# Modulation products on column quarters, 64 slots for the first expert, and the expert order ahead of its gather

## The chip, the cores and the metric

The kernel runs on one core of a Trainium2 chip. The metric is device time of one execution in microseconds (us), a median of several runs. Five engines work side by side: TensorE (PE; its weight loads are shown as PEld), VectorE (DVE), ScalarE (ACT), GpSimd (POOL) and SyncE (SP), which here does little but issue loads from memory. A program has one queue of instructions for each engine; engines wait for each other by semaphores.

## The reference, cut to what matters

Three transformer layers on 256 tokens of 1024 columns, in float32. The change is in layer 1 (and in a helper that layer 3 uses too). Layer 1 computes a modulation of six parts from one vector `c`, a mixer, and a mixture of 32 experts, of which each token takes four:

```python
mod = jax.nn.silu(c) @ w_ada[l] + b_ada[l]                  # [1024] @ [1024, 6144]
sh1, sc1, gt1, sh2, sc2, gt2 = [m[:, None, :] for m in jnp.split(mod, 6, axis=-1)]
h = rms_norm(x, g_pre_mix[l]) * (1 + sc1) + sh1
y = hybrid_mixer(h, ...)
x = x + gt1 * rms_norm(y, g_post_mix[l])
h = rms_norm(x, g_pre_ffn[l]) * (1 + sc2) + sh2
y = moe_ffn(h, w_router[l], ...)      # top_k of 32, softmax, per expert: @ w_mlp1, swiglu, @ w_mlp2
x = x + gt2 * rms_norm(y, g_post_ffn[l])
```

Layer 2 has another mixer and a dense feed-forward part, layer 3 a modulation of its own, attention, and 32 smaller experts. The router decides at run time how many of the 256 tokens an expert gets.

## The kernel before

**Modulation.** `Ada` holds `silu(c)` as 8 columns of 128 (`c[:, k]`), and works on `w_ada` in 24 tiles of 1 MiB, each with 8 blocks (k) of 128 rows by 256 columns, for 256 values of the modulation. `Ada.tile(n, pe)` does the first `pe` blocks on TensorE, as a product with one column of `c` (L301, a single row of 256 as the result), and the others on VectorE as multiplications and additions into an accumulator of 128 rows (L304, L306). `Ada.columns` turns the result into two columns of 128: the accumulator and the row are summed by small products with ones (L325), and VectorE adds the bias (L329). Layer 1's parts (1, 0) come with four blocks on each engine, ahead of the mixer; the parts 2, 4 and 3 entirely on VectorE, woven into the mixer; the last four tiles by `Fill` (L365), as single rows on TensorE between the steps of norm and router. Layer 3 calls `Ada.tile` with all 8 blocks on TensorE for six of its tiles, and leaves the others to VectorE.

**Order of the experts.** Expert 0 is always done first. The 31 others are put into places 1 to 31 by how many tokens they got. `Order.keep` copies the mask of the choices (on GpSimd, L1171), `Order.make` counts, ranks (a matrix `perm`), sorts the biases by place (L1231) and then writes the list of expert numbers `ids` (L1194 on TensorE, L1195 on VectorE). `Order.expert` reads an entry of it into a register of SP (L1221), which the address of a load needs.

**Slots.** A place has room for `CAPS` tokens: places 0 to 4 have 128 slots, the next eleven 64, the others 32. `gather` collects the tokens of a group of places by products with a 0/1 matrix (L1305, L1306). What exceeds a place's slots is done by `overflow1` at the end, behind a branch.

**Experts.** Each has 12 weight tiles of 1 MiB: 8 of `w_mlp1`, 4 of `w_mlp2`, issued by SP (L134) into a ring of 12 slots. `Expert1.product` (L1556) makes the 4 products of a tile, the tokens being stationary and the weights moving; with 64 slots the two halves of the result lie on two column halves of the engine, with 32 slots on four column quarters. Between the tiles `step` and `advance` weave the gathers of the next group, the activation, and the scatter of the expert before. Ten tiles of expert 0 are issued ahead of the first load that needs `ids`.

**Order of the work.** In most of the mixer a scheduler orders each engine's queue; from the norm after it to the first expert, and again from the second expert on, the order on TensorE, VectorE and ScalarE is that of the code.

Of the kernel before, what the change touches and what calls it, by code (L numbers as in the profile page):

```python
# [31 lines left out]
class Kern:  # L32
# [21 lines left out]
    def constants(self):  # L54

        nc, pool = self.nc, self.perm
        self.ident = self.cload("ident", [P, P], pool)
# [220 lines left out]
class Ada:  # L278
# [13 lines left out]
    def tile(self, n, pe, wv=None):  # L292


        K, nc = self.K, self.K.nc
        wv = (K.wtile(K.a[self.w][n]) if wv is None else wv).rearrange("p (k n) -> p k n", k=KD)
        terms, ps = [], None
        if pe:
            ps = K.bank()[0:1, :256]
            for k in range(pe):  # L300
                nc.tensor.matmul(ps, self.c[:, k:k + 1], wv[:, k], start=k == 0, stop=k == pe - 1)  # L301
        if pe < KD:
            acc = self.pool.tile([P, 256], F32, tag="acc", name="acc")
            nc.vector.tensor_scalar(acc, wv[:, pe], self.c[:, pe:pe + 1], None, op0=ALU.mult)  # L304
            for k in range(pe + 1, KD):
                nc.vector.scalar_tensor_tensor(acc, wv[:, k], self.c[:, k:k + 1], acc, op0=ALU.mult, op1=ALU.add)  # L306
            terms.append((acc, K.ones[:, 0:1]))
        return n, terms, ps

    def column(self, n, terms, row):  # L310
        weave(self.columns(n, terms, row))

    def columns(self, n, terms, row):

        K, nc = self.K, self.K.nc
        if row is not None:
            acc = self.pool.tile([P, 256], F32, tag="acc", name="acc")[0:1]
            nc.scalar.copy(acc, row)
            terms.append((acc, K.ones[0:1, 0:1]))
        yield  # L320
        yield
        ps = K.bank()
        for j in range(2):
            for i, (acc, one) in enumerate(terms):
                nc.tensor.matmul(ps[:, j:j + 1], acc[:, 128 * j:128 * j + 128], one, start=i == 0, stop=i == len(terms) - 1)  # L325
        for _ in range(6):
            yield
        m = slice(2 * n, 2 * n + 2)
        nc.vector.tensor_add(self.mod[:, m], ps[:, :2], self.b[:, m])  # L329
# [5 lines left out]
    def tiles(self, ns, pe=lambda n: 0):  # L335
        last = None
        for n in ns:
            t = self.tile(n, pe(n % 4))
# [6 lines left out]
    def steps(self, parts, pe=lambda n: 0):  # L345
# [3 lines left out]
class Fill:  # L349
# [9 lines left out]
    def go(self, m):  # L359
        K = self.ad.K  # L360
        for _ in range(min(m, KD * len(self.ns) - self.next)):
            i, k = divmod(self.next, KD)
            if k == 0:
                self.ps.append(K.bank()[0:1, :256])
# [2724 lines left out]
```

## Time and profile before

| | us |
|---|---|
| median of 3 runs | 2215.63 |
| lowest, highest | 2211.54, 2216.04 |
| profiled execution | 2217.96 |
| its span in the trace | 2216.1 |

| engine | busy, us | share |
|---|---|---|
| PE | 2008.4 | 91% |
| DVE | 994.4 | 45% |
| ACT | 639.2 | 29% |
| POOL | 135.8 | 6% |

The stages in the trace: modulation and first norm 0 to 44.5, mixer to 165.1, norm, router and first gather to 197, experts of layer 1 to 1173, layer 2 and the mixer of layer 3 to about 1900, its experts to 2187, and the end. A share of busy time over the whole span is a mean over these stages; the rows below are read stage by stage. "Idle before" is the time in which an engine did nothing just ahead of an instruction, with what ended it. The clock of TensorE is given as a share of its full speed (PEclk).

### The profile page before, as it was taken

To read this page: it belongs to the slowest core of one execution; us is meant where nothing else is said; L and a number is where in the kernel's file an instruction comes from. 1 tells how busy PE (TensorE), PEld (TensorE's weight loads), DVE (VectorE), ACT (ScalarE), POOL (GpSimd) and SP (SyncE) were. 2 spreads that over 40 slices of the span, in tenths; PEclk is the share of its full clock that TensorE was granted. 3 is DMA by queue.
4 is the path that set the end of the run, shared out by engine and by line. 5 is a ranking of instruction groups with operands and counts; after the bars stand their busy time and mean duration, and the time that the engine had idled before them with its cause. 6 is when DMAs were issued, how large, how long until landed. Compare 5 with 4: busy or idle time off the path is not lost. (4 is left out here: it accounts for less than half of the span.)

```text
span 2216.1 us, 31702 instructions
## 1 busy us (share of the span) xinstructions
PE 2008.4 (91%) x12454; PEld 1255.3 (57%) x12454; DVE 994.4 (45%) x2096; ACT 639.2 (29%) x1162; POOL 135.8 (6%) x199
## 2 busy tenths in 40 slices
PE   7899999988988898879976978999999999899996
PEld 4785434332423243223415956999778999556664
DVE  5783322221222222222225997788565854323334
ACT  3553101110101001010104583444454543322221
POOL 4000000000000000000000001000200000000000
PEclk9999999999999999999997988999999999899998
DMA  7665899999999999999995523577442554799991
GB/s 290 238 246 203 362 420 410 420 419 419 420 419 419 419 420 419 419 419 420 419 419 212 201 84 133 213 281 284 164 149 101 196 177 147 297 362 395 397 399 43
DMA packets 97807, 680.08 MB, mean 307 GB/s; under 512 B 11760, under 2 KB 14064, under 8 KB 16112
## 3 DMA queue, kind: packets, MB, share of 16 engines
q1 hardware_dynamic: 94752, 671.00, 76.1%
q0 software_dynamic: 2320, 6.41, 1.0%
q8 instruction: 102, 1.67, 0.3%
q10 hardware_dynamic: 576, 0.53, 0.1%
q14 instruction: 57, 0.47, 0.1%
HBM read 675.79 MB, written 2.11 MB: 306 GB/s over the span
## 5 line engine op out<-in xcount | busy, mean ns | idle before, releaser
L1556 PE MATMUL bank<-w,xg 128*32 128x512 f32 (+2 forms) x2048 | 460.3, 626 | 65.1 <-DMA w<-w_mlp 64.9
L1556 PEld LDWEIGHTS bank<-w,xg 128*32 128x32 f32 (+2 forms) x2048 | 131.2, 135 | 323.6 <-issue 188.7
L167 DVE TENSOR_TENSOR whl<-w,whl 128x1024 fp32r<-128x1024 f32 (+1 forms) x211 | 251.4, 1199 | 136.2 <-ACT whl L166 135.9
L166 ACT CAST whl<-w 128x1024 fp32r<-128x1024 f32 (+1 forms) x219 | 221.5, 1029 | 229.9 <-PE bank L417 99.9
L1556 PE MATMUL bank<-w,a 128*32 128x512 f32 (+2 forms) x1024 | 256.0, 610 | 24.7 <-DMA w<-w_mlp 24.7
L1586 ACT COPY us<-bank 128x512 f32<-128x512 f32 x64 | 37.5, 585 | 527.8 <-PE bank L1556 527.8
L1641 DVE TENSOR_TENSOR sg<-bank,b1cols 128x128 f32<-128x128 f32 (+2 forms) x64 | 25.6, 400 | 361.6 <-PE bank L1593 200.4
L1556 PEld LDWEIGHTS bank<-w,a 128*32 128x32 f32 (+2 forms) x1024 | 67.3, 131 | 141.4 <-issue 93.7
L1352 DVE TENSOR_TENSOR moe<-moe,bank 128x512 f32<-128x512 f32 x128 | 82.3, 684 | 119.4 <-PE bank L1347 108.4
L415 PE MATMUL bank<-hh,whl 128*128 128x256 f32 x448 | 129.0, 288 | 0.0
L417 PE MATMUL bank<-hh,whl 128*128 128x256 f32 x448 | 126.8, 283 | 2.1 <-DVE whl L167 2.1
L416 PE MATMUL bank<-hl,whl 128*128 128x256 f32 x448 | 126.8, 283 | 0.0
L2944 PE MATMUL bank<-w,xg 128*64 128x256 f32 x1024 | 118.5, 384 | 0.0
L306 DVE SCALAR_TENSOR_TENSOR acc<-w,siluc,acc 128x256 f32<-128x256 f32 x234 | 115.0, 499 | 4.5
L417 PE MATMUL bank<-xh,whl 128*128 128x256 f32 x400 | 113.1, 283 | 2.2 <-DVE whl L167 2.2
L415 PE MATMUL bank<-xh,whl 128*128 128x256 f32 x400 | 113.2, 284 | 0.8 <-ACT xh L1860 0.8
L416 PE MATMUL bank<-xl,whl 128*128 128x256 f32 x400 | 113.2, 283 | 0.0
L2762 DVE TENSOR_TENSOR moe<-moe,bank 128x512 f32<-128x512 f32 x60 | 39.8, 684 | 149.9 <-PE bank L2989 149.9
L2944 PEld LDWEIGHTS bank<-w,xg 128*64 128x64 f32 x1024 | 70.8, 138 | 37.7 <-issue 3.6
L417 PEld LDWEIGHTS bank<-hh,whl 128*128 128x128 f32 x448 | 85.0, 190 | 3.1 <-DVE whl L167 3.1
L415 PEld LDWEIGHTS bank<-hh,whl 128*128 128x128 f32 x448 | 85.3, 190 | 0.9 <-issue 0.6
L416 PEld LDWEIGHTS bank<-hl,whl 128*128 128x128 f32 x448 | 85.2, 190 | 0.6 <-issue 0.5
(721 smaller groups left out, 3519.8 us busy)
## 6 DMA issues: line engine op xcount, KB each, us to landing
w<-w_mlp SPq DMA_DIRECT2D x384, 1024.0 KB, 19.8
w<-w SPq DMA_DIRECT2D x96, 1024.0 KB, 7.7
w<-w_ada SPq DMA_DIRECT2D x48, 1024.0 KB, 5.4
w<-w_in SPq DMA_DIRECT2D x48, 1024.0 KB, 4.8
w<-w_ff SPq DMA_DIRECT2D x32, 1024.0 KB, 4.9
w<-w_out SPq DMA_DIRECT2D x12, 1024.0 KB, 4.9
w<-cmp_w SPq DMA_DIRECT2D x4, 1024.0 KB, 4.7
w<-w_ret_o SPq DMA_DIRECT2D x4, 1024.0 KB, 4.8
```

The lines of the kernel that those rows point to most:

```text
L166: nc.scalar.copy(h, src)
L167: (eng or nc.vector).tensor_tensor(l, src, h.bitcast(F32), op=ALU.subtract)
L306: nc.vector.scalar_tensor_tensor(acc, wv[:, k], self.c[:, k:k + 1], acc, op0=ALU.mult, op1=ALU.add)
L415: nc.tensor.matmul(out, w.h[k][:, c], x.h[:, k], start=first and k == 0, stop=False)
L416: nc.tensor.matmul(out, w.h[k][:, c], x.l[:, k], start=False, stop=False)
L417: nc.tensor.matmul(out, w.l[k][:, c], x.h[:, k], start=False, stop=last and k == nk - 1)
L1352: nc.vector.tensor_add(out[:, t, c], out[:, t, c], ps[n])
L1556: self.K.nc.tensor.matmul(out[n % self.banks][r:r + cap], x[:, k], w[:, k % 2, 512 * n:512 * n + 512], start=k < m, stop=k >= KD - m)
L1586: (nc.scalar.copy, nc.vector.tensor_copy)[n](us[:, n], u[n])
L1641: nc.vector.tensor_tensor(o, ps, v.rearrange("p (c a) -> p c a", a=1).broadcast_to([P, 4, cap]), op=ALU.add)
L2762: nc.vector.tensor_add(out[:, k:k + 2], out[:, k:k + 2], ps)
L2944: nc.tensor.matmul(self.u[64 * n:64 * n + 64], self.xg[:, k], w[:, j, n], start=k == 0, stop=k == KD - 1)
```

## The change

Four things. (1) A modulation tile of layer 1 is no longer shared with VectorE nor done as a single row. All 8 blocks are products on TensorE, `dot`, with the column of `c` broadcast to 32 columns: block k writes the 32 rows of quarter k modulo 4 of a result of 128 by 256. ScalarE copies this result (`kept`), two products with the identity turn it, and VectorE sums the four quarters and adds the bias. `Fill` does the same. The identity is loaded ahead of the first tile's columns. Layer 3's tiles that are done on TensorE become quarters too; its others stay on VectorE. (2) Place 0 has 64 slots instead of 128, and `Order.make` writes its limit accordingly. (3) `Order.keep` and the first part of `Order.make` come directly after the choice of the experts; `ids` is written ahead of expert 0's gather, the sorted biases after it. (4) The splits of the tokens for the gather (`tok.l_of`) and the first steps of that gather are put in other places between the last modulation products.

```diff
@@ class Ada
-        if pe:
-            ps = K.bank()[0:1, :256]
-            for k in range(pe):
-                nc.tensor.matmul(ps, self.c[:, k:k + 1], wv[:, k], start=k == 0, stop=k == pe - 1)
-        if pe < KD:
-            acc = self.pool.tile([P, 256], F32, tag="acc", name="acc")
-            nc.vector.tensor_scalar(acc, wv[:, pe], self.c[:, pe:pe + 1], None, op0=ALU.mult)
-            for k in range(pe + 1, KD):
-                nc.vector.scalar_tensor_tensor(acc, wv[:, k], self.c[:, k:k + 1], acc, op0=ALU.mult, op1=ALU.add)
-            terms.append((acc, K.ones[:, 0:1]))
-        return n, terms, ps
+        if pe:
+            ps = K.bank()[:, :256]
+            for k in range(KD):
+                self.dot(ps, wv, k)
+            return n, True, ps
...
+    def dot(self, ps, wv, k):
+        r = slice(32 * (k % 4), 32 * (k % 4) + 32)
+        self.K.nc.tensor.matmul(ps[r], self.c[:, k:k + 1].broadcast_to([P, 32]), wv[:, k], start=k < 4, stop=k >= KD - 4)
...
+    def kept(self, ps):
+        acc = self.pool.tile([P, 256], F32, tag="acc", name="acc")
+        self.K.nc.scalar.copy(acc, ps)
+        return acc
...
         for j in range(2):
-            for i, (acc, one) in enumerate(terms):
-                nc.tensor.matmul(ps[:, j:j + 1], acc[:, 128 * j:128 * j + 128], one, start=i == 0, stop=i == len(terms) - 1)
+            if quarters:
+                transpose_to(K, ps[:, 128 * j:128 * j + 128], acc[:, 128 * j:128 * j + 128])
+            else:
+                nc.tensor.matmul(ps[:, j:j + 1], acc[:, 128 * j:128 * j + 128], K.ones[:, 0:1], start=True, stop=True)
...
+            nc.vector.reduce_sum(self.mod[:, m], ps[:, :256].rearrange("p (j g r) -> p j g r", j=2, g=4)[:, :, :, 0], axis=AX.X)
+            nc.vector.tensor_add(self.mod[:, m], self.mod[:, m], self.b[:, m])
@@ class Fill, go
-                self.ps.append(K.bank()[0:1, :256])
-            K.nc.tensor.matmul(self.ps[i], self.ad.c[:, k:k + 1], self.w[i][:, k], start=k == 0, stop=k == KD - 1)
+                self.ps.append(K.bank()[:, :256])
+            self.ad.dot(self.ps[i], self.w[i], k)
@@ mix1
-    mods = ad.steps((1, 0), lambda n: 4)
+    mods = ad.steps((1, 0), True)
+    K.ident = K.cload("ident", [P, P], K.perm)
...
-        weave(att, linear(), ad.steps((2, 4)), also)
+        weave(att, linear(), ad.steps((2, 4), True), also)
...
-        weave(output(), ad.steps((3,)))
+        weave(output(), ad.steps((3,), True))
@@
-CAPS = [WIDE] * WIDES + [NARROW] * NARROWS + [SLIM] * (E1 - WIDES - NARROWS)
+CAPS = [NARROW] + [WIDE] * (WIDES - 1) + [NARROW] * NARROWS + [SLIM] * (E1 - WIDES - NARROWS)
@@ Order.make
-        bias_columns(K, b1, self.perm.bitcast(F32), self.b1)
-
-        yield
+        yield
+
         ps = K.bank()
         nc.tensor.matmul(ps[0:1, :n], K.iota_p[:n], perm, start=True, stop=True)
         nc.vector.tensor_copy(self.ids, ps[0:1, :n])
+        yield
+        bias_columns(K, b1, self.perm.bitcast(F32), self.b1)
+        yield
...
+        nc.vector.tensor_scalar(more, pos, 0.0, float(NARROW - WIDE), op0=ALU.is_equal, op1=ALU.mult)
+        nc.vector.tensor_tensor(cap, cap, more, op=ALU.add)
@@ the mixture of experts, layer 1
+            order.keep(best.mask)
             R = Routes(K, rt, best.mask, E1, lambda: tok.l_of(0))
+            made = order.make(K, rt, R, b1)
+            next(made)
             fill.go(32)
-            order.keep(best.mask)
-            tok.l_of(1)
...
             step()
+            tok.l_of(1)
+            next(made)
             tok.l_of(2)
             tok.l_of(3)
+            step(4)
             fill.columns()
             fill.copy()
             fill.columns()
...
-            step(3)
...
-                            made = order.make(K, rt, R, b1)
                             next(made)
```

TensorE's queue around the first expert, before (L1067 to L1071 are the routing, L365 the last modulation tiles, L1305 and L1306 expert 0's gather, L1556 its products, L1179 and L1181 the counts of `Order.make`, L1231 its biases; a row's last numbers are the result's shape and how often it stands):

```order
L1071 MATMUL bank<-topm,ones 1x32
L365 MATMUL bank<-w,siluc_90 1x256 x11
L325 MATMUL bank<-ones,acc 128x1 x8
L1305 MATMUL bank<-oh,tokh 128x128
L1306 MATMUL bank<-oh,tokl 128x128
...
L1556 MATMUL bank<-w,xg 128x512 x4
...
L1179 MATMUL bank<-mask_1688,ones 128x32 x2
L1181 MATMUL bank<-ones,mask_1688 128x1 x2
L1556 MATMUL bank<-w,xg 128x512 x2
L1231 MATMUL bank<-perm,b_360 128x32 x16
```

The same place of the same queue after (L1080 routing, L1188 and L1190 the counts, L309 the modulation quarters, L1202 the list `ids`, L1318 and L1319 the gather, L556 the turning, L1571 expert 0's products, L1244 the biases):

```order
L1080 MATMUL bank<-topm,ones 1x32
L1188 MATMUL bank<-mask_1708,ones 128x32 x2
L1190 MATMUL bank<-ones,mask_1708 128x1 x2
L309 MATMUL bank<-w,siluc_90 32x256 x11
L1202 MATMUL bank<-perm,iota_p 1x32
L1318 MATMUL bank<-oh,tokh 128x64
L1319 MATMUL bank<-oh,tokl 128x64
...
L556 MATMUL bank<-ident,acc 128x128 x8
L1571 MATMUL bank<-w,xg 64x512 x4
...
L1244 MATMUL bank<-perm,b_344 128x32 x8
```

The counts and the list stand behind the routing and ahead of the gather, where before the counts stood behind the fourth of expert 0's products and the list (L1194) further back.

TensorE's queue in the mixer, before (L325 are the sums of a modulation tile that VectorE accumulated, L1781, L794 and L804 the mixer's own work):

```order
L417 MATMUL bank<-hh,whl 128x256
L325 MATMUL bank<-ones,acc 128x1 x2
L1781 MATMUL bank<-bmr,flip 128x512
L794 MATMUL bank<-state,qe_615 64x128 x4
...
L804 MATMUL bank<-v,AT 64x128 x16
L325 MATMUL bank<-ones,acc 128x1 x2
```

The same place after (L309 are the 8 quarter products of a modulation tile, L556 its turning):

```order
L425 MATMUL bank<-hh,whl 128x256
L309 MATMUL bank<-w,siluc_90 32x256 x8
L556 MATMUL bank<-ident,acc 128x128 x2
L1796 MATMUL bank<-bmr,flip 128x512
...
L813 MATMUL bank<-v,AT 64x128 x16
L309 MATMUL bank<-w,siluc_90 32x256 x8
```

A tile's 8 products and two turning products stand between full-width products of the mixer, in place of two products with ones.

VectorE's queue at the softmax of the mixer's attention, before (L696, L697 and L700 are its sum, reciprocal and scaling, L304 and L306 modulation tiles):

```order
L304 TENSOR_SCALAR acc<-w,siluc_90 128x256
L306 SCALAR_TENSOR_TENSOR acc<-w,siluc_90,acc 128x256 x4
L696 TENSOR_TENSOR sm<-sm,es 128x8
L306 SCALAR_TENSOR_TENSOR acc<-w,siluc_90,acc 128x256
L697 RECIPROCAL sm<-sm 128x8
...
L700 TENSOR_SCALAR s<-s,sm 128x128 x4
```

And after (L336 and L337 are the sum of the quarters and the bias):

```order
L336 TENSOR_REDUCE modw_ada<-bank 128x2
L337 TENSOR_TENSOR modw_ada<-modw_ada,b_ada 128x2
L705 TENSOR_TENSOR sm<-sm,es 128x8
L706 RECIPROCAL sm<-sm 128x8
L709 TENSOR_SCALAR s<-s,sm 128x128 x4
```

The accumulations between the three steps of the softmax are gone from this queue.

## Rows read from the trace of the kernel before

**Rows 1.** Windows by stage: window, length, busy per engine, PEclk, DMA share, GB/s.

```profile
0.00:44.50 44.50, 32.10 (x134) 17.10 (x134) 25.81 (x64) 13.75 (x28) 17.58 (x33) 0.98 0.88 314
44.50:165.10 120.60, 112.81 (x818) 96.18 (x819) 94.92 (x227) 63.76 (x128) 13.42 (x16) 0.95 0.66 237
165.10:197.00 31.90, 30.54 (x182) 17.96 (x180) 16.07 (x50) 13.55 (x31) 1.05 (x3) 0.98 0.91 362
197.30:229.30 32.00, 32.00 (x134) 18.69 (x134) 6.91 (x30) 6.64 (x19) 2.10 (x2) 0.91 0.03 5
229.30:1171.70 942.40, 843.23 (x4342) 314.89 (x4340) 230.82 (x526) 106.99 (x226) 74.87 (x126) 0.97 1.01 418
1927.50:2187.00 259.50, 255.40 (x1879) 162.54 (x1878) 79.62 (x177) 60.02 (x162) 0.00 (x0) 0.99 0.86 341
```

**Rows 2.** Waits of SP, 160 to 260: line, waited for, total us, times, longest.

```profile
SPq L1221 <- DVE ids L1195: 47.3, 1, 47.3
```

**Rows 3.** Timeline around 226 (start, length, work), and loads issued 226 to 230.

```profile
226.40 0.18 DVE L1195 CAST ids<-bank 1x32 int32<-1x32 f32 x1 [0.94 <-PE bank L1194]
227.77 33.22 SPq L134 DMA_DIRECT2D w<-w_mlp  x16
...
DMA to landing us min/median/max: 4.9/7.7/10.6
```

**Rows 4.** Windows within the experts of layer 1, columns as in rows 1.

```profile
300.00:350.00 50.00, 50.00 (x174) 20.81 (x173) 12.75 (x27) 4.24 (x9) 5.95 (x6) 1.00 1.01 418
...
450.00:500.00 50.00, 41.31 (x280) 16.21 (x279) 11.41 (x27) 7.50 (x17) 2.45 (x6) 0.91 1.01 419
```

**Rows 5.** PE groups by shape, 229 to 1175: rows*columns, moving, count | busy, mean ns.

```profile
L1556 PE MATMUL bank<-w,xg 128*64 128x512 f32 x704 | 167.8, 603 | 30.1 <-DMA w<-w_mlp 30.1
L1556 PE MATMUL bank<-w,xg 128*32 128x512 f32 x1024 | 145.9, 647 | 33.1 <-DMA w<-w_mlp 32.9
L1556 PE MATMUL bank<-w,xg 128*128 128x512 f32 x279 | 124.7, 598 | 1.9 <-DMA w<-w_mlp 1.9
L1556 PE MATMUL bank<-w,a 128*32 128x512 f32 x512 | 97.8, 618 | 14.7 <-DMA w<-w_mlp 14.7
```

**Rows 6.** Expert 0's products alone (L1556): window, length, PE and PEld busy.

```profile
196.99:251.99 55.00, 39.86 (x81) 14.78 (x81) 0.95 0.43 175
```

**Rows 7.** End of the first stage: PE timeline, and a window as in rows 1.

```profile
36.37 1.89 PE L301 MATMUL bank<-w,siluc 128*1 128x256 f32 x8
...
44.51 0.58 PE L417 MATMUL bank<-hh,whl 128*128 128x256 f32 x1 [2.08 <-DVE whl L167]
...
35.00:44.50 9.50, 6.30 (x35) 4.43 (x34) 9.29 (x24) 6.16 (x13) 3.48 (x3) 0.89 0.63 225
```

**Rows 8.** Mixer, 44.5 to 165.1: two groups as in rows 5, one wait of PE.

```profile
L306 DVE SCALAR_TENSOR_TENSOR acc<-w,siluc,acc 128x256 f32<-128x256 f32 x84 | 38.4, 479 | 1.1
L325 PE MATMUL bank<-ones,acc 128*128 128x1 f32 x40 | 5.2, 235 | 0.0
PE bank L548 <- ACT s L702: 6.0, 1, 6.0
```

**Rows 9.** Routing, 165 to 197: a PE group, and the PE timeline.

```profile
L548 PE MATMUL bank<-ident,hf 128*128 128x128 f32 x16 | 2.2, 280 | 0.0
...
187.98 4.91 PE L365 MATMUL bank<-w,siluc 128*1 128x256 f32 x22
```

**Rows 10.** Layer 3: timeline of PE and DVE, and a wait of SP from 1935 on.

```profile
1569.16 3.61 PE L301 MATMUL bank<-w,siluc 128*1 128x256 f32 x16
...
1571.47 0.81 DVE L2337 TENSOR_SCALAR xn<-xn,lnmv,lnrs 128x1024 f32<-128x1024 f32 x1
...
1902.84 5.17 PE L301 MATMUL bank<-w,siluc 128*1 128x256 f32 x16 [4.98 <-DMA w<-w_ada]
...
1952.19 3.62 PE L301 MATMUL bank<-w,siluc 128*1 128x256 f32 x16
...
SPq L134 <- PE bank L2944: 145.6, 55, 8.1
```

More of the change, by code (lines that the diff above doesn't have):

```diff
@@ L56, in constants @@
         nc, pool = self.nc, self.perm
-        self.ident = self.cload("ident", [P, P], pool)
         self.iota = self.cload("iota", [P, P], pool)
@@ L290, in __init__, with tile, column, columns @@
         self.mod = pool.tile([P, 48], F32, name="mod" + w)
-    def tile(self, n, pe, wv=None):
+    def tile(self, n, pe):
         K, nc = self.K, self.K.nc
-        wv = (K.wtile(K.a[self.w][n]) if wv is None else wv).rearrange("p (k n) -> p k n", k=KD)
-        terms, ps = [], None
+        wv = K.wtile(K.a[self.w][n]).rearrange("p (k n) -> p k n", k=KD)
         if pe:
-            ps = K.bank()[0:1, :256]
-            for k in range(pe):
-                nc.tensor.matmul(ps, self.c[:, k:k + 1], wv[:, k], start=k == 0, stop=k == pe - 1)
-        if pe < KD:
-            acc = self.pool.tile([P, 256], F32, tag="acc", name="acc")
-            nc.vector.tensor_scalar(acc, wv[:, pe], self.c[:, pe:pe + 1], None, op0=ALU.mult)
-            for k in range(pe + 1, KD):
-                nc.vector.scalar_tensor_tensor(acc, wv[:, k], self.c[:, k:k + 1], acc, op0=ALU.mult, op1=ALU.add)
-            terms.append((acc, K.ones[:, 0:1]))
-        return n, terms, ps
-    def column(self, n, terms, row):
-        weave(self.columns(n, terms, row))
-    def columns(self, n, terms, row):
+            ps = K.bank()[:, :256]
[3 more added lines that the diff above has]
+        acc = self.pool.tile([P, 256], F32, tag="acc", name="acc")
+        nc.vector.tensor_scalar(acc, wv[:, 0], self.c[:, 0:1], None, op0=ALU.mult)
+        for k in range(1, KD):
+            nc.vector.scalar_tensor_tensor(acc, wv[:, k], self.c[:, k:k + 1], acc, op0=ALU.mult, op1=ALU.add)
+        return n, False, acc
+    def dot(self, ps, wv, k):
+        r = slice(32 * (k % 4), 32 * (k % 4) + 32)
+        self.K.nc.tensor.matmul(ps[r], self.c[:, k:k + 1].broadcast_to([P, 32]), wv[:, k], start=k < 4, stop=k >= KD - 4)
+    def column(self, n, quarters, acc):
+        weave(self.columns(n, quarters, acc))
+    def kept(self, ps):
+        acc = self.pool.tile([P, 256], F32, tag="acc", name="acc")
+        self.K.nc.scalar.copy(acc, ps)
+        return acc
+    def columns(self, n, quarters, acc, kept=False):
         K, nc = self.K, self.K.nc
[L316 to L319, printed above, removed]
+        if quarters and not kept:
+            acc = self.kept(acc)
         yield
@@ L328, in columns, with tiles @@
         m = slice(2 * n, 2 * n + 2)
-        nc.vector.tensor_add(self.mod[:, m], ps[:, :2], self.b[:, m])
+        if quarters:
+            nc.vector.reduce_sum(self.mod[:, m], ps[:, :256].rearrange("p (j g r) -> p j g r", j=2, g=4)[:, :, :, 0], axis=AX.X)
+            nc.vector.tensor_add(self.mod[:, m], self.mod[:, m], self.b[:, m])
+        else:
+            nc.vector.tensor_add(self.mod[:, m], ps[:, :2], self.b[:, m])
     def part(self, i):
         return self.mod[:, 8 * i:8 * i + 8]
-    def tiles(self, ns, pe=lambda n: 0):
+    def tiles(self, ns, pe=False):
         last = None
         for n in ns:
-            t = self.tile(n, pe(n % 4))
+            t = self.tile(n, pe)
             if last:
@@ L343, in tiles, with steps @@
         self.column(*last)
-    def steps(self, parts, pe=lambda n: 0):
+    def steps(self, parts, pe=False):
         return self.tiles([4 * i + n for i in parts for n in range(4)], pe)
@@ L370, in copy @@
         for i in range(len(self.acc), self.next // KD):
-            acc = self.ad.pool.tile([P, 256], F32, tag="acc", name="acc")[0:1]
-            self.ad.K.nc.scalar.copy(acc, self.ps[i])
-            self.acc.append(acc)
+            self.acc.append(self.ad.kept(self.ps[i]))
     def columns(self):
         for i in range(self.done, len(self.acc)):
-            self.ad.column(self.ns[i], [(self.acc[i], self.ad.K.ones[0:1, 0:1])], None)
+            weave(self.ad.columns(self.ns[i], True, self.acc[i], True))
         self.done = len(self.acc)
```

## Prediction

> **What bounds the kernel now.** I read the windows by stage first [rows 1]. Of 2216.1 us, the stretch from 229.3 to 1171.7 is the mixture of experts of layer 1: there the DMA engines are busy all the time (share 1.01, 418 GB/s), and TensorE is not (843 of 942 us). So this stretch ends when the last weight tile has landed, and what matters is when its stream begins. Ahead of it stand 32.0 us, from 197.3 to 229.3, with a DMA share of 0.03. The waits of SP, which issues the weight loads, tell why [rows 2]: it waits 47.3 us once, at L1221, for the list of expert numbers `ids`. Only expert 0's loads are known without it. The list is cast at 226.40 and the first load that needs it is issued at 227.77, 1.37 later [rows 3]. TensorE meanwhile works off expert 0, and is behind its weights until about 350; from then on it waits for tiles (50.00 busy of 50.00 in 300 to 350, 41.31 in 450 to 500) [rows 4]. A hole in the stream that is closed is therefore given back whole at 1172, if TensorE doesn't hold up the stream in another place. In front of the stream, TensorE is the bound: 112.81 busy of 120.60 from 44.5 to 165.1 [rows 1]. Behind it, from 1927.5 on, the experts of layer 3 keep TensorE busy 255.40 of 259.50, and SP waits for it (145.6 us at L134 for the products of L2944): there TensorE's own work is the bound [rows 1, 10].
>
> **Price of a quarter tile.** Eight products of 256 columns in four quarters are, in columns, four products of 512 in four quarters, and that is what one weight tile of a 32-slot expert is: eight records of the form 128*32. Its busy time is 145.9/1024 = 0.142 per record, against 124.7/279 = 0.447 for 128*128 and 167.8/704 = 0.238 for 128*64 [rows 5]. So 8 x 0.142 = 1.14 us per tile. I take this row as it is nearest in shape. The upper neighbour is the second product of these experts, 97.8/512 = 0.191, so 1.53 a tile; the far bound is that nothing overlaps, 3.62 us, as a whole tile takes today on one column [rows 10]. The column step after it is even: two transposes cost four records of 2.2/16 = 0.14, the ones products before four of 5.2/40 = 0.13 [rows 8, 9].
>
> The dearer row of the two is the one broken up more by full-width work. The Trainium skill, TensorEngine Tiling (Array Packing), section Key Properties, says that a change of the tiling mode drains TensorE; by that every one of the quarter tiles, which now stand between full-width products, would pay twice. By 1.53 instead of 1.14 for the ten tiles that count below the sum would be 4 us worse. The trace has the sign of it, but doesn't show that the drain is the cause.
>
> **Start, 0 to 44.5.** The eight first modulation tiles had four products each on TensorE and four on VectorE. From 35.0 to 44.5 VectorE is busy 9.29 of 9.50 us and TensorE, done with the last tile's products at 36.37 + 1.89, waits for it, at the end 2.08 us for a split weight [rows 7]. VectorE loses all eight tiles. What is late next is the last of the tiles themselves: the engines of the DMA are busy 0.88 of this stage [rows 1]. I take -8 us, between -5 and -10.
>
> **Mixer, 44.5 to 165.1.** Twelve tiles move from VectorE (84 + 12 operations, 38.4 us for the 84 [rows 8]) to TensorE. VectorE wasn't the bound, so its relief is worth little; TensorE is. Twelve times 1.14 = 13.7. Two of the twelve stand ahead of the one long wait of TensorE here, 6.0 us for the softmax on ScalarE [rows 8], and are hidden in it: 11.4 stay. In that wait, two accumulations stand on VectorE between the softmax's sum and its scaling, about 0.46 each (38.4/84): -1. A copy on ScalarE per tile lies beside other work. Sum +10, between +4 (if more is hidden) and +14 (at 1.53).
>
> **Routing, 165.1 to 197.** Of the four last tiles 11 products stand in front of expert 0's gather: 4.91 us [rows 9], now 11 x 0.142 = 1.6, so -3.3. The two mask products and the one for `ids` add some 0.6. Together -2.7, between 0 and -4. So expert 0's first product moves by -8 + 10 - 2.7, from 196.99 [rows 6] to about 196.3. `ids` now hangs on the routing alone: the routing products stand ahead of the row at 187.98 [rows 9], then come five short steps on VectorE and two on TensorE, so 191 to 192, and the first load with 1.37 more at about 193. The load queue would run dry at 197.3: some 4 us of cover. The wait for `ids` stands in SP's queue behind expert 0's loads as before.
>
> **Experts of layer 1.** The hole is 32.0 us. What takes its place is the ring of 12 slots. In the order of the loads tiles 1 to 10 are expert 0's, and tile 22 can be issued only when tile 10 is used, at the end of these ten. Its ten tiles with what is woven in took 55.0, of which 39.86 are its own 81 records [rows 6]. At 64 slots 80 x 0.238 = 19.0, plus the other 15.1: 34.1, rather less, since its gather is half as wide; say 32. From 196.3 that is 228.3. The stream by then wants tile 21 at 197.3 + 11 x 2.51 = 224.9 (1 MiB at 418 GB/s is 2.51) and tile 22 at 227.4; issued at 228.3, and with the 4.9 from issue to landing that the shortest load of an empty queue took [rows 3], it comes at 233.2. So 6 of the 32 are lost again: -26. With 28 for expert 0 it would be -30, with 34.1 and some of the order's matrices in the way -20. Every microsecond by which expert 0 starts later than 196.3 is one less: the start, the mixer and the routing count only through this, and are in the 26.
>
> **Layer 3.** Six tiles that were whole on one column become quarters, each 3.62 to about 1.14. Two among the experts, the first at 1952.19: 2 x 2.5 = -5.0, since TensorE is the bound. One at 1902.84, which waits for its weights, with the router behind it: its 5.17 shrink [rows 10]; I take the -2.5 of a tile at full clock. The two ahead of the attention are hidden: the second half of the layer norm is ready only at 1571.47 + 0.81 = 1572.28, and the first tile ends at 1569.16 + 3.61 = 1572.77 [rows 10]; -0.4. The last one, after the router, waits for the routing anyway. Sum -8, between -3 and -9.
>
> **Sum.** -26 - 8 = -34: from the profiled 2217.96 to 2184. The median is 2.3 below the profiled execution, so 2182 on its scale, which is the forecast; the rivals' times below are on this scale too.
>
> **Rivals.**
> Serial quarters, slower: if the four quarters didn't run at the same time, a tile would cost 3.62. The mixer would pay 10 x 3.62 - 1 = +35, the start and routing would gain nothing, expert 0 would begin 35 later than before, 36 later than in my sum, and the experts would lose 10 instead of gaining 26; layer 3 would be even: +10, 2226. It decides at a tile price of about 3.1 (44 us of the sum for 2.48 us of price is 17.7 for one, and 34/17.7 = 1.9 above 1.14). Against it stand 1728 records of 64 and 32 columns at a half and a third of the full price [rows 5].
> Ring instead of list: the hole becomes a row of waits for slots, since order, biases and the next gathers all stand between expert 0's tiles. -18 for the experts, in all -26: 2190.
> The list still late: it hangs on something behind expert 0. Then only the 64 slots help: 226.40 is 29.4 after the first product; at 32/55 of that, 17.1, the first load would be issued at 214.8 instead of 227.77, -13, in all -21: 2195. For it: the load waits for semaphores of other engines and queues too. Against it: by the order, all of these belong to work of the mixer and the norm after it, ahead of the routing.
> All better: tiles cheaper, more hidden in the mixer, stalls of 2 only. -42: 2174.
>
> **Chances.** The forecast, 2177 to 2188, 0.52; ring 0.18; list late 0.05; all better 0.14; serial 0.05; something unnamed 0.06, spread over the three signs. From these: faster by over 0.2% (4.4 us, about what a measurement of this kernel can tell from none) 0.92, within it 0.03, slower 0.05. The range from 2171 to 2198 takes in the bounds of the ring, the mixer and layer 3, and leaves out the serial case.
>
> **What would show it.** Right: SP's wait at the list falls below 5 us; the DMA share from 197 to 229 is above 0.7; the last expert tile of layer 1 lands near 1146; a quarter tile's 16 records take 1.0 to 1.5 us; the first product of expert 0 stands between 194 and 199; the two tiles in layer 3 are followed by an end that is 5 us nearer. Wrong: a tile at over 2 us; TensorE idle in the mixer for the copies on ScalarE; waits of SP for slots of over 10 us in all between 200 and 260; or TensorE behind its weights so far, in the experts of 128 slots, that the stream stops there.

## The result and the profile after

The changed kernel takes 2193.41 us (median of 6 runs, 2192.31 to 2200.81) against 2215.84 for the kernel before: a ratio of 0.9913, 95% interval 0.9901 to 0.9924, 22.4 us less. The profiled execution takes 2192.83, its span is 2191.0. The sign and the range were right; the likeliest forecast, 2182 with 2177 to 2188 of its own, was not reached. Of the cases that were named, the late list (2195) is nearer by its number, but the list came early; by its mechanism it is the one with the ring in the place of the list (2190, with -18 for the experts, where -15.6 was measured).

The windows by stage of the kernel after stand beside [rows 1]: window, length, busy time and records of PE, PEld, DVE, ACT and POOL, PEclk, DMA share, GB/s.

```profile
0.00:41.10 41.10, 20.33 (x151) 8.48 (x151) 13.56 (x40) 12.68 (x25) 17.50 (x33) 0.80 0.91 339
41.10:167.90 126.80, 122.04 (x974) 98.26 (x974) 60.15 (x143) 67.22 (x139) 12.86 (x16) 0.97 0.66 233
167.90:195.80 27.90, 24.21 (x200) 15.67 (x200) 17.78 (x66) 14.26 (x34) 1.06 (x3) 0.94 0.99 384
197.30:229.30 32.00, 32.00 (x152) 16.31 (x149) 5.38 (x25) 6.27 (x16) 1.25 (x2) 0.84 0.70 257
229.30:1156.10 926.80, 830.70 (x4301) 305.75 (x4299) 226.22 (x516) 104.72 (x221) 73.76 (x126) 0.97 1.01 416
1910.00:2170.00 260.00, 254.53 (x1881) 161.79 (x1879) 83.23 (x181) 60.49 (x158) 0.00 (x0) 0.99 0.86 344
```

The hole from 197.3 to 229.3 is filled, but not whole: a DMA share of 0.70 where there was 0.03. TensorE is busy without a gap in it, as before. The list is there early, and SP's waits from 150 to 260 (line, waited for, total us, times, longest) are those of a queue that waits for slots instead:

```profile
192.59 0.17 DVE L1203 CAST ids<-bank 1x32 int32<-1x32 f32 x1
193.94 0.36 SPq L133 DMA_DIRECT2D w<-w_mlp  x1
```

```profile
SPq L133 <- PE bank L1571: 43.9, 18, 4.8
SPq L133 <- PE bank L556: 14.2, 3, 6.4
SPq L1234 <- DVE ids L1203: 12.1, 1, 12.1
SPq L133 <- PE bank L1329: 8.0, 1, 8.0
```

`ids` came 33.8 us earlier than in [rows 3]; the one wait of 47.3 [rows 2] is now 12.1 and lies beside a queue that still has loads in flight; but 43.9 us went into 18 waits for a ring slot, which the products of the experts (now L1571) set free. The eleventh tile, the first that needs the list, landed at 199.5 instead of 232.6; tile 22, the first that needs a slot of expert 0 back, at 241.2 instead of 261.4; the last tile at 1156.14 instead of 1171.70. Of 33 us gained at the list, 20 are left at tile 22 and 15.6 at the end of the stage. The windows from 200 on show where the rest went (columns as above):

```profile
200.00:210.00 10.00, 10.00 (x61) 7.63 (x60) 0.00 (x0) 2.23 (x8) 0.00 (x0) 0.79 0.74 289
210.00:220.00 10.00, 10.00 (x43) 3.90 (x39) 1.40 (x4) 2.29 (x3) 0.91 (x2) 0.70 0.59 200
220.00:230.00 10.00, 10.00 (x47) 4.51 (x47) 2.85 (x16) 2.10 (x6) 0.34 (x1) 1.00 0.78 300
230.00:240.00 10.00, 10.00 (x90) 4.96 (x89) 3.12 (x9) 2.15 (x6) 1.25 (x2) 1.00 0.91 326
```

TensorE is never idle here, and its clock falls in the middle: at the lower level, 1.2 of 2.4 GHz, from 206 to 216. The products of expert 0 alone (L1571; window, length, PE and PEld busy, PEclk, DMA share, GB/s), to be read beside [rows 6]:

```profile
195.79:238.02 42.23, 25.15 (x81) 5.78 (x81) 0.88 0.75 275
```

Its ten tiles took 42.2 us instead of 55.0; the forecast had them at 32.

### The profile page after: what moved, and what is told of

The parts are those of the page before. It is cut to its first block, busy times and chain, and to the rows that moved or that the text cites. A ratio compares the mean times of both kernels' runs of the same rounds, so it can differ in the third digit from the quotient of the medians.

```text
span 2191.0 us, 31927 instructions
## 1 busy us (share of the span) xinstructions
PE 1970.8 (90%) x12614; PEld 1227.5 (56%) x12614; DVE 944.6 (43%) x1998; ACT 641.0 (29%) x1172; POOL 133.2 (6%) x199
## 5 line engine op out<-in xcount | busy, mean ns | idle before, releaser
L1571 PE MATMUL bank<-w,xg 128*32 128x512 f32 (+2 forms) x2048 | 447.1, 628 | 63.8 <-DMA w<-w_mlp 63.3
L1571 PEld LDWEIGHTS bank<-w,xg 128*32 128x32 f32 (+2 forms) x2048 | 123.7, 133 | 319.0 <-issue 185.6
L1571 PE MATMUL bank<-w,a 128*32 128x512 f32 (+2 forms) x1024 | 253.2, 619 | 23.4 <-DMA w<-w_mlp 23.4
L1656 DVE TENSOR_TENSOR sg<-bank,b1cols 128x128 f32<-128x128 f32 (+2 forms) x64 | 25.1, 392 | 371.3 <-PE bank L1608 203.8
L1571 PEld LDWEIGHTS bank<-w,a 128*32 128x32 f32 (+2 forms) x1024 | 64.0, 131 | 140.0 <-issue 92.7
L425 PEld LDWEIGHTS bank<-xh,whl 128*128 128x128 f32 x400 | 76.0, 190 | 2.7 <-DVE whl L166 2.7
```

The lines of the kernel that those rows point to most:

```text
L425: nc.tensor.matmul(out, w.l[k][:, c], x.h[:, k], start=False, stop=last and k == nk - 1)
L1571: self.K.nc.tensor.matmul(out[n % self.banks][r:r + cap], x[:, k], w[:, k % 2, 512 * n:512 * n + 512], start=k < m, stop=k >= KD - m)
L1656: nc.vector.tensor_tensor(o, ps, v.rearrange("p (c a) -> p c a", a=1).broadcast_to([P, 4, cap]), op=ALU.add)
```

## The experiments

Two accounts were at odds. By the first, which the expectations below call the pace, the stream of weights now follows TensorE: what counts is how long expert 0 takes, and the list is out of the way. By the second, the hole, it still counts when `ids` is there, and 64 slots alone do little. The fourth part of the change (where `tok.l_of` and the gather's first steps stand) has no experiment of its own; it goes back together with the list. Times of all experiments are set against the kernel before, run on the same chip. "First product" is expert 0's, "ten tiles" the time from it to the end of its tiles, "last tile" the landing of layer 1's last expert tile: 195.79, 42.2 and 1156.14 in the kernel after.

**The list late again** (64 slots and quarters stay):

```diff
@@ Order.make
-        yield
+        bias_columns(K, b1, self.perm.bitcast(F32), self.b1)
         ...
-        yield
-        bias_columns(K, b1, self.perm.bitcast(F32), self.b1)
-        yield
@@ the mixture of experts, layer 1: order.keep, Order.make, l_of(1) where they stood in the kernel before
```

> The changed kernel with the list of experts, the counts and the biases put back to their old places behind the first tiles of expert 0; 64 slots and quarter products stay. Theory 'pace': after the hole is closed, TensorE's time for expert 0 and its successors, which gives the ring's slots free, sets the weight stream until about 400 us, and the early list is worth little. Then the list comes some 18 us after expert 0's first product, the stream starts near 216 instead of 199 and catches up while TensorE works: last tile of layer 1 at 1156 to 1160, 2193 to 2197 us. Rival 'hole': what paid was the list; the 17 us by which the stream starts later stay, last tile near 1170, 2207 us.

Measured: 2203.18, ratio 0.9948 (0.9931 to 0.9965). Both accounts missed; it lies between them. `ids` came at 220.14, 6.3 earlier than in the kernel before, and the last tile landed at 1165.06, 6.6 earlier: with a late list the 6.3 at `ids` come back as 6.6 at the end of the stage. SP waits for the list as before, and TensorE, with its 64 slots done soon, stands without weights from 275 on. SP from 150 to 260, PE from 197 to 420, in this kernel, and then PE in the kernel after:

```profile
SPq L1232 <- DVE ids L1204: 39.7, 1, 39.7
```

```profile
PE bank L1567 <- DMA w<-w_mlp: 8.6, 14, 1.5
```

```profile
PE bank L1571 <- DMA w<-w_mlp: 3.4, 6, 0.6
```

In the kernel after TensorE waits for no weights until 402.8 (before: 425.8). So the list binds when it is late, and TensorE when it is early.

**128 slots for expert 0 again** (early list and quarters stay):

```diff
-CAPS = [NARROW] + [WIDE] * (WIDES - 1) + [NARROW] * NARROWS + [SLIM] * (E1 - WIDES - NARROWS)
+CAPS = [WIDE] * WIDES + [NARROW] * NARROWS + [SLIM] * (E1 - WIDES - NARROWS)
```

> The changed kernel with 128 slots for expert 0; early list and quarter products stay. Theory 'pace': expert 0 takes some 13 us more on TensorE, nearly all of which comes back at the end: last tile at 1167 to 1170, 2205 us. Rival 'hole': the stream starts near 199 all the same, so only a few us are lost: last tile at 1158 to 1160, 2196 us.

Measured: 2206.46 (2205.28 to 2217.36), ratio 0.9970 (0.9957 to 0.9983), by the median as the pace had it. The list is there at 192.87, and nearly nothing comes of it: the ten tiles end at 249.24, 53.2 after the first product, and tile 22 lands at 252.3. The last tile, forecast for 1167 to 1170, landed at 1178.01; but the traced execution was the slowest of ten (2217.36), with a half clock from 250 to 271 (shown in the last section), so this landing is not that of the median.

**Quarters only** (128 slots and late list, the two edits above together):

> The quarter products alone: 128 slots for expert 0 and the list at its old place. The late list alone cost 10 us (2203), the 128 slots alone 13 (2206). Theory 'two bounds': the experts of layer 1 start as the later of two things lets them, the weight stream behind the list and TensorE behind expert 0; undoing one makes it the bound, undoing the other as well adds little. Then 2206 to 2210, last tile of layer 1 near 1171. Rival 'sum': both losses add, 2193 + 10 + 13 = 2216, as slow as the kernel before.

Measured: 2208.28 (2204.40 to 2220.19), ratio 0.9957 (0.9941 to 0.9974). The last tile, forecast near 1171, landed at 1181.10, again in the slowest execution (2220.19, half clock from 254 to 274). With it the table is full, medians in us, all four with quarters:

| | 128 slots | 64 slots |
|---|---|---|
| list late | 2208.3 | 2203.2 |
| list early | 2206.5 | 2193.4 |

By the medians one alone is worth 2 or 5 us, neither of which is clear of the intervals (0.9970 and 0.9948 against 0.9957), and both together 15, which is (0.9913). This is what two bounds in one place look like: the stream can't go on before the later of the list and the slots. Neither is the cause of the gain by itself.

**Old modulation** (64 slots and early list stay, all modulation as in the kernel before):

```diff
@@ class Ada, Fill, mix1: the "-" lines of the change's diff again
-    mods = ad.steps((1, 0), True)
+    mods = ad.steps((1, 0), lambda n: 4)
```

> 64 slots and the early list, with the old modulation everywhere (four blocks on each engine, then VectorE, single rows in layer 1's last four tiles and in layer 3). From the traces the quarters gained 3.5 us ahead of the mixer, lost 5 in it, gained 2 to 3 in the routing and 9 in layer 3: expert 0 begins within 1 us of 195.8, and the end is 9 us later than in the changed kernel, 2202. Rival: the first three are worth more than that together, over 2206.

Measured: 2204.59, ratio 0.9953 (0.9937 to 0.9970). So the quarters are worth 11 us here. From the end of layer 1's experts on TensorE to the end of the span it takes 1041.2 us, against 1033.7 with quarters: 7.5 of them are layer 3's. In layer 1 the first product stands at 196.78, only 1.0 later, and the last tile lands 3.6 later (1159.76). The other 2.6 fall in between, where the half clock lasts from 206 to 220 in this execution instead of from 206 to 216.

**Rows in layer 3** (its six tiles on one column again):

```diff
@@ Ada.tile
+        if pe == KD:
+            ps = K.bank()[0:1, :256]
+            for k in range(KD):
+                nc.tensor.matmul(ps, self.c[:, k:k + 1], wv[:, k], start=k == 0, stop=k == KD - 1)
+            return n, "row", ps
```

> The changed kernel with the six modulation tiles of layer 3 as single rows again, 3.62 us each; all else stays. If these six are worth what the comparison of the traces says (2.6 at the router, 2 x 2.5 among the experts, the first two hidden), it is 8 to 9 us slower, 2202 us. Rival: most of that shift comes from elsewhere in layer 3 (clock, weights), then 3 us or less, 2196 us.

Measured: 2200.68, ratio 0.9941 (0.9921 to 0.9961), 7.3 above the kernel after. Layer 1 is unchanged (last tile at 1155.60), and from the end of its experts to the end it takes 1040.2 instead of 1033.7: 6.5, beside the 7.5 above. That is layer 3's share, as far as single traces give it: in the traces of the eight other experiments, which all have the quarters there, the same stretch takes 1033.3 to 1037.1.

**First eight tiles as before** (four blocks on TensorE, four on VectorE):

```diff
-    mods = ad.steps((1, 0), True)
+    mods = ad.steps((1, 0), 4)
```

> The changed kernel with the first eight modulation tiles done as before (four blocks on TensorE as a row, four on VectorE); the others stay quarters. The traces give these quarters 3.5 us at the mixer's first steady product (44.51 before, 41.06 after), where the prediction had 8. If the 3.5 are theirs, the mixer starts at 44.5 again and the end is 3 to 4 us later, 2197. Rival: the 3.5 come from the lighter start of VectorE and the weights' arrival, or are eaten by a half clock of 20 us in place of 7, then 2193.

Measured: 2196.08 (2193.91 to 2204.86), ratio 0.9929 (0.9901 to 0.9956): by the median not to be told from the kernel after. In the traces the product that ends the first stage stands at 41.64 instead of 41.06, and with the old modulation everywhere at 41.35. The start, from which -8 was expected, got 3.5 us, and the quarters gave 0.3 to 0.6 of these. The rival's half clock is there too: 24.8 to 45.3 in the kernel after, 39.6 to 46.5 here, so what the quarters would give at the same clock isn't shown.

**The mixer's twelve tiles on VectorE again:**

```diff
-        weave(att, linear(), ad.steps((2, 4), True), also)
+        weave(att, linear(), ad.steps((2, 4)), also)
...
-        weave(output(), ad.steps((3,), True))
+        weave(output(), ad.steps((3,)))
```

> The changed kernel with the twelve modulation tiles of the mixer back on VectorE; the first eight, the last four and those of layer 3 stay quarters. Theory 'pace': the mixer is TensorE's, 12 tiles at 1.0 us are off its path, some of them hidden before, so expert 0 begins 5 us earlier (near 191) and the end comes 4 to 5 us earlier, 2188 us. Rival: the weight stream of the experts is held by the DMA engines, the 5 us are lost there, 2193 us.

Measured: 2192.07 (2186.39 to 2194.40), ratio 0.9895 (0.9866 to 0.9924). The median doesn't separate it from the kernel after. In the trace the first product comes 3.4 earlier (192.42), and the last tile 4.3 earlier (1151.82): so this part of the change costs 3 to 4 us in layer 1. TensorE's wait for the softmax, in the mixer (kernel after, then this kernel), is the place where a part of its price was hidden:

```profile
PE bank L556 <- ACT s L711: 2.4, 1, 2.4
```

```profile
PE bank L556 <- ACT s L711: 6.4, 1, 6.4
```

**No bias products.** The pace account was then asked what slows expert 0. Ahead of the half clock of the kernel after (from 205.7) stand the products that sort the biases, 32 records of 32x32, and the first of sixteen 64-wide products of a gather. In the timeline of the kernel after (start, length, engine, line, work):

```profile
200.17 1.97 PE L1244 MATMUL bank<-perm,b 32*128 32x32 f32 x16
202.07 1.08 PE L1571 MATMUL bank<-w,xg 128*64 128x512 f32 x4
203.07 1.97 PE L1244 MATMUL bank<-perm,b 32*128 32x32 f32 x16
```

```diff
-        bias_columns(K, b1, self.perm.bitcast(F32), self.b1)
+        nc.gpsimd.memset(self.b1, 0.0)
```

> The changed kernel without the 16 products that sort the biases of w_mlp1 by place; these biases are set to zero by GpSimd, so experts 1 to 31 lack them. The products take 3.8 us on TensorE, and behind them its clock is at half for some 10 us in every kernel looked at. Theory 'pace': TensorE sets the stream there, so these 3.8 us and, if the products bring the clock down, some 4 to 5 more come back: 2185 to 2190, granted clock above 0.9 from 200 to 220. Rival: the half clock belongs to the start of the experts, whatever stands there: it stays, 2190. Rival 'DMA': nothing comes back, 2193.

Measured: 2191.44 (2183.76 to 2195.14), ratio 0.9881 (0.9854 to 0.9907): by the time neither forecast nor rivals can be told apart. (The "some 10 us in every kernel" of the expectation holds for three of the five kernels traced by then beside that before; it was 6.8 with rows in layer 3 and 3.4 with 128 slots.) The clock stays at 1.00 from 200 to 230, and the ten tiles take 33.4 us, nearly the 32 of the forecast. But in the profiled execution (2195.11) the half clock then comes at 232 to 256, and the last tile lands at 1157.17, no earlier than in the kernel after (windows as above):

```profile
220.00:230.00 10.00, 10.00 (x90) 5.14 (x86) 1.66 (x5) 2.74 (x7) 1.24 (x2) 1.00 0.90 336
240.00:250.00 10.00, 10.00 (x30) 2.65 (x22) 1.39 (x3) 0.58 (x1) 0.00 (x0) 0.50 0.73 270
```

What was gained in expert 0's ten tiles was lost in those behind them. Two of its runs, at 2183.76 and 2187.78, are some 7 to 11 below the other two.

**Bias products in turn.** The two halves of the biases lie on different rows of the array and in different banks; here their products alternate, all computed:

```diff
@@ bias_columns
-    for half in range(2):
-        ...
-        for j in range(8):
-            K.nc.tensor.matmul(ps[:, j], b1[r, 128 * j:128 * j + 128], sel[r], start=True, stop=True)
+    for j in range(8):
+        for half in range(2):
+            r = slice(E1 * half, E1 * half + E1)
+            K.nc.tensor.matmul(pss[half][:, j], b1[r, 128 * j:128 * j + 128], sel[r], start=True, stop=True)
```

> The changed kernel with one edit: the bias products of the two halves are issued alternately, on different rows of TensorE and into two banks. In the kernel with the mixer on VectorE this took 1.6 us from these products, and the half clock behind them was gone. Theory: half a clock for 10 us inside expert 0 costs 5 us on TensorE, and the experts' start gives it back whole: last tile of layer 1 near 1149, 2187 us, no clock under 0.9 from 200 to 220. Rival: the clock kept up there because the mixer had been on VectorE; here it falls as before, and only 1.6 us are gained, 2192.

Measured: 2191.14 (2186.70 to 2192.50), ratio 0.9887 (0.9867 to 0.9906). The products run two at a time:

```profile
204.23 1.97 PE L1244 MATMUL bank<-perm,b 32*128 32x32 f32 x30
```

Thirty records (of 32; two are missing from the trace) take what sixteen took. There is no half clock from 200 to 340, the ten tiles take 35.8 (-6.4) and the last tile lands at 1152.52 (-3.6), although the first product stood 2.7 later in this execution, after a half clock at 178 to 185 and 192 to 195. Against the kernel after the median is 2.3 lower, within the spread of both. (Behind layer 1 this execution took 1037.1 where the kernel after took 1033.7, so that the 3.6 were lost again.) So the clock did as the theory said, and the time did not: 2187 was forecast, and 2191 is nearer to the rival. Of the 6.4 at the ten tiles 3.4 are the same 81 records at full clock (25.15 and 21.74); the shorter bias products, up to 1.9, are a part of the rest, so the clock alone isn't worth the whole.

**Both: mixer on VectorE, bias products in turn.**

> The changed kernel with the mixer's twelve modulation tiles on VectorE and the bias products issued alternately for the two halves, which lie on different rows of the engine, into two banks. By 'pace' the mixer gives 4, the bias products become shorter by up to 1.9: 2187. Rival: pairs don't overlap and the clock falls as before: 2189 to 2190.

Measured: 2185.86 (2184.33 to 2187.19), ratio 0.9869 (0.9852 to 0.9885). As forecast. All four of its runs are below all six of the kernel after, and the two intervals of the ratio don't meet, so it beats both kernels. First product at 193.34, ten tiles 35.8, tile 22 at 232.8, last tile at 1147.06. Its windows, and its products of expert 0 alone (L1572):

```profile
197.30:229.30 32.00, 32.00 (x226) 17.05 (x226) 6.18 (x26) 8.75 (x22) 2.50 (x4) 1.00 0.87 327
```

```profile
200.00:210.00 10.00, 10.00 (x73) 5.84 (x71) 0.64 (x2) 2.08 (x7) 0.00 (x0) 1.00 0.85 315
210.00:220.00 10.00, 10.00 (x48) 4.55 (x48) 3.70 (x18) 3.55 (x7) 1.25 (x2) 1.00 0.90 342
```

```profile
193.34:229.12 35.78, 21.73 (x81) 5.11 (x81) 1.00 0.86 320
```

With the clock at 1.00 the same 81 records take 21.73 instead of 25.15, and the stream gets a share of 0.87 of the 32 us instead of 0.70. The last tile is 9.1 earlier than in the kernel after; with the mixer's 4.3 taken off, 4.8 of the 10.4 that the forecast of the experts was short of come back when expert 0 keeps its clock and the bias products are up to 1.9 shorter.

## Why the prediction was right in sign and too large in size

**The price of a quarter tile: right.** 1.14 was taken, 1.07 measured (1.93 at half clock):

```profile
167.93 1.07 PE L309 MATMUL bank<-w,siluc 128*32 128x256 f32 x16
1885.29 1.93 PE L309 MATMUL bank<-w,siluc 128*32 128x256 f32 x16 [4.94 <-DMA w<-w_ada]
1887.15 4.29 PE L1045 MATMUL bank<-hf,w 128*36 128x256 f32 x16
```

The tile at 167.93 is a whole one among full-width work. The dearer row, 0.191 a record, which had been set beside the drain of the Trainium skill (TensorEngine Tiling (Array Packing), Key Properties), would have made it 1.53. No such extra is to be seen in the 1.07; the first record stands 0.32 behind the full-width one ahead of it (167.61), where these follow each other at 0.23, so what a change of mode can add there is at most about 0.1; what the runs don't show is whether a drain is there and lies beside other work. The case of serial quarters fell by the same row. The turning, taken as four records of 0.14, is two in the trace, 0.44 a tile.

**Start: -8 forecast, -3.5 measured** (the product that ended the first stage stood at 44.51, now at 41.06). The step that failed is what was to be late next. VectorE and TensorE both were relieved, and the weight of the norm's product still waits 1.80:

```profile
41.06 0.58 PE L425 MATMUL bank<-hh,whl 128*128 128x256 f32 x1 [1.80 <-DVE whl L166]
```

The last of the eight modulation tiles landed at 33.2, in the kernel before at 32.7, though it was issued 7.6 us earlier: the start is paced by the DMA (share 0.91), and TensorE, which from 14 us on waited for no tile before, now waits 6.7 us for five of them. The prediction had named this and priced it too low. Since 41.35 was reached with the old modulation too, most of even the 3.5 isn't the quarters' doing. The traces show where it was lost. The same three groups of TensorE, in the kernel before and with the old modulation:

```profile
16.27 2.12 PE L325 MATMUL bank<-ones,acc 128*128 128x1 f32 x8
18.33 2.08 PE L386 MATMUL bank<-sq,ones 128*128 128x256 f32 x4
20.34 2.63 PE L301 MATMUL bank<-w,siluc 128*1 128x256 f32 x8
```

```profile
15.61 1.31 PE L324 MATMUL bank<-ones,acc 128*128 128x1 f32 x8
16.85 1.13 PE L385 MATMUL bank<-sq,ones 128*128 128x256 f32 x4
17.91 1.89 PE L300 MATMUL bank<-w,siluc 128*1 128x256 f32 x8
```

They took 6.83 us and 4.33: in the traced execution of the kernel before, TensorE's records ran at about half speed until 22 us, with the old modulation until 15. (The record of the granted clock begins only at these two times; the windows show 1.00 for what lies ahead of it.) So some 2.5 of the 3.5 us belong to a slow beginning of that one execution, and why it was slow stays open.

**Mixer: +10 forecast, +7.4 measured** (from the end of the first stage to the first product of the last four tiles, which `Fill` does: 121.5 before and 128.9 after):

```profile
166.00 3.62 PE L365 MATMUL bank<-w,siluc 128*1 128x256 f32 x16
```

```profile
169.99 1.07 PE L309 MATMUL bank<-w,siluc 128*32 128x256 f32 x16
```

In these two stretches TensorE is busy 113.7 us and 123.9, so its work grew by 10.2 where 13.7 were forecast, and its idle time shrank by 2.8. The wait for the softmax, 6.0 in [rows 8], took in 3.6 us; the prediction had allowed about that, two tiles (2.3) and 1 for VectorE's accumulations. What it had too high is the work: 12 x 1.07 = 12.8 instead of 13.7, and the two stretches differ in their half clock (11.5 us before and 7.6 after), worth some 2 us by an estimate from the two levels; no run shows that the change brought this about. (The expectation of the old modulation has 5 and 2 to 3 for the mixer and the routing: that is what comes out when 167.93, the mixer's twelfth tile, is taken for the first of the last four.)

**Routing: -2.7 forecast, -5.2 measured** (from there to expert 0's first product, 31.0 before and 25.8 after). Only the 11 of the 32 last products that stand behind the routing had been priced, 4.91 then and 1.50 now. The other 21 shrank as well, from 10.0 us to 5.4, of which some went into a longer wait for VectorE at the norm (2.2 instead of 0.5).

The errors of the start (4.5 too much), the mixer (2.6 too much) and the routing (2.5 too little) nearly cancel: the first product of expert 0 stood at 195.79, for 196.3 forecast, and the first load at 193.94, for "about 193". That is luck, not a confirmation of the three terms.

**Experts of layer 1: -26 forecast, -15.6 measured. This is the term that was mis-sized**, and in it the step "34.1, rather less, since its gather is half as wide; say 32". The ten tiles took 42.2. The mechanism was the one described, tile 22 waits for the end of expert 0's tiles: forecast end 228.3 and landing 233.2, measured 238.0 and 241.2. By the runs the 10 us of the ten tiles are made up so: the 81 records take 21.7 at full clock (in the kernel with both edits), not 80 x 0.238 = 19.0, since they are broken up by other work: +2.7. At half clock for 10 us they take 25.15: +3.4. The rest, what is woven in, took 42.23 - 25.15 = 17.1 instead of the 13 that "say 32" left for it: +4, of which the half clock has a part; in the kernel with both edits it is 35.8 - 21.7 = 14.1. So tile 22 landed 8.0 later than forecast.

The second error stands behind it: of the 20.2 gained at tile 22, 14.7 are left at tile 27, 13.2 at tile 40, and 15.6 at the last one. (Together 12.6; of the 28.2 that its own landing of 233.2 was ahead of the kernel before, the prediction had counted 26.) Expert 0's ten tiles are followed by those of a place with 32 slots (records 128*32 from 238.02 on), by expert 0's last two and by the products woven between them, and TensorE sets the pace there too: the loads of the tiles 22 to 27 were issued at 236.3 to 250.8, 2.9 each where a tile takes the DMA 2.5, and the DMA is not busy throughout before 260:

```profile
240.00:250.00 10.00, 10.00 (x52) 3.01 (x48) 3.42 (x8) 0.59 (x1) 0.00 (x0) 1.00 0.86 329
250.00:260.00 10.00, 10.00 (x68) 3.42 (x68) 4.08 (x10) 1.58 (x3) 0.82 (x2) 1.00 0.97 347
```

With both edits the loss behind tile 22 is the same in kind: 28.6 gained there (it landed at 232.8, for 233.2 forecast, with the first product 3.0 earlier than forecast), and 24.6 at the last tile. The prediction had read that TensorE stays behind its weights until 350 [rows 4], and yet priced the pace through expert 0's ten tiles alone.

Of its signs of being right, the tile's price and the first product came true; the DMA share came to 0.70, the bound itself, and the last tile landed at 1156.1 instead of near 1146. The sign of being wrong that it had given itself for this, "waits of SP for slots of over 10 us in all", came true with 43.9. One of the signs of being right, a wait at the list "below 5 us", was badly chosen: 47.3 less the 34 by which the list was to come earlier is 13, and 12.1 is what it was, at no cost: tile 11 landed 2.5 behind tile 10 (199.5 and 197.0), the step of a full stream.

**Layer 3: -8 forecast, -7.5 and -6.5 by the two experiments** (-9.0 from the traces of before and after, of which 1.6 also came with the old modulation: 1041.2 against 1042.8 from the end of the experts on). Since this stretch varies by up to 3.8 us between traces that share its program, -8 can't be told from any of these. The steps were the ones named: the two tiles among the experts at 1.07 instead of 3.62, the one ahead of the router at half clock (1.93 for the 5.17 of [rows 10], which was a half-clock tile in part), and the two ahead of the attention hidden:

```profile
1933.27 1.07 PE L309 MATMUL bank<-w,siluc 128*32 128x256 f32 x16
```

**The sum**: -16.1 at the end of layer 1's experts on TensorE and -9.0 behind it are the -25.1 of the two spans; the medians differ by 22.4, since the profiled execution of before lies 2.1 above its median and that of after 0.6 below. The whole range, 2171 to 2198, was met because it had taken in the bounds of the ring.

## What to carry to other kernels

Before a wait is removed, ask not only when the next thing in the queue could start, but who sets its pace from then on; here the list and TensorE's pace were two bounds in one place, so that easing one gave 5 us at most and easing both gave 15. Follow the pace past the first place where it binds: a third of the loss stood behind it. Where an engine is shown busy without a gap, count what it does there with records from the same stretch, broken up as they are there, not with the mean of a stretch in which it runs in peace. And where work moves onto the busy engine, look for the waits in which it hides: 3.6 us of the mixer's 12 tiles went into one.

## What the runs showed of the hardware

In a stretch in which TensorE's records follow each other without a gap, the granted clock fell to 0.50, the lower level, for 7 to 24 us, at a place that changed with what stood ahead of it: 206 to 216 in the kernel after and 206 to 220 with the old modulation, behind or among the bias products (for 6.8 us, 207.5 to 214.3, with rows in layer 3, whose layer 1 is the same program as that of the kernel after); 250 to 271 with 128 slots and an early list, 254 to 274 with quarters only, 232 to 256 without bias products, each behind 44 small products of the next experts' gather and two of the ranks. With 128 slots and an early list (windows as above):

```profile
250.00:260.00 10.00, 10.00 (x29) 1.89 (x28) 2.48 (x5) 0.00 (x0) 0.00 (x0) 0.52 0.68 246
260.00:270.00 10.00, 10.00 (x22) 2.97 (x19) 1.38 (x2) 0.59 (x1) 0.00 (x0) 0.50 0.68 245
```

An estimate from the two levels: where TensorE sets the pace, half of such a stretch is lost, 3 to 12 us. The times of one kernel can lie at two levels: those of 128 slots with an early list at 2205 to 2207 (six) or at 2211 to 2217 (four). The profiled one, with the half clock above, took 2217.36; no faster one was traced, so that the clock makes this difference isn't shown. Nor is it shown that the small products bring the half clock about: with the bias products in turn no such stretch stood there in two kernels, and without them it came later, behind the next small ones; but the same 44 stand at 236.20 in the kernel after, and no half clock follows until 356. What sets it off stays open. Another one goes with the quarters of the first eight tiles: all nine kernels that have them show 20 to 24 us of half clock between 19 and 47 (24.8 to 45.3 in the kernel after, where TensorE waits for weights between the tiles), and the three without them 7 us, which begin at 39 to 42. A second surprise is that the bias products, on 32 rows of the array each and in two banks, ran at 30 records in the time of 16 merely by taking turns.
